# A two-layer recurrent decoder step on one core: norm statistics by a product with ones, the first embedding projection moved to the start, and the state-space constants made in pieces

## The chip, the core and the metric

The kernel runs on one core of a Trainium2 chip. The metric is the device time of one execution in microseconds (us). The profile shows five engines that run their own instruction lists and wait for each other through semaphores: TensorE (PE: matmuls, with its weight loads shown apart as PEld), VectorE (DVE), ScalarE (ACT), GpSimd (POOL) and SyncE (SP), which here does nothing but issue transfers. Matmul results go into PSUM, everything else is in SBUF or in the chip's main memory (DRAM).

## The reference

One step of a decoder trunk with two layers over 576 columns: 512 positions of a prompt and 8 samples of 8 positions. The width is 1024. Each layer is a mixer, a squared-ReLU MLP and a gated embedding addition, each behind a norm:

```
def rmsnorm(x, g):
    y = x * rsqrt(mean(x * x, axis=-1) + EPS)
    return y * g

for i in range(2):
    hn = rmsnorm(h, norm_mix[i])
    h = h + mixer_i(hn)                       # layer 0: mLSTM and retention; layer 1: HGRN2 and S5
    hn = rmsnorm(h, norm_ff[i])
    h = h + square(relu(hn @ w_ff1[i])) @ w_ff2[i]
    gate = sigmoid(rmsnorm(h, norm_ple[i]) @ w_ple_gate[i])
    h = h + gate * (p[i] @ w_ple_proj[i])     # p[i]: an input, 256 wide
y = rmsnorm(h, norm_final)
```

The S5 half of layer 1 is a complex diagonal state space of 32 groups with 64 states: from A, log_dt, B and C it needs the powers of exp(dt A), the scaled B, and products of them. These are constants: they hang on no activation.

## The kernel before

h is held transposed, as eight tiles of 128 rows (features) by 576 columns. Every large product is one of 219 *units*: 512 KB of weights that SP fetches (`wr`, L223), that ACT copies into a rounded part `wh` (L226), and whose remainder `wl` DVE or POOL forms (L227). Activations are split in the same way into `xh` (ACT, L270, with the norm's weight g multiplied in) and `xl` (DVE, L271). Each product is then three matmuls (wh·xh, wh·xl, wl·xh, L235) for each of two halves of 288 columns, into a `pb` bank of PSUM. One output tile of 128 rows with 1024 inputs is 48 matmuls, one with 256 inputs is 12.

The norm's factor r is not needed by the matmul, since it is a number for each column: it is multiplied in when the result leaves PSUM (for the MLP: `fu` L398 on DVE, relu times r, then ACT squares it, L399, and it is split again into `uh` and `ul`, L267 and L268). So the statistic is computed beside the first matmuls that use the norm. ACT squares the eight tiles (L304), POOL and DVE add them up into two tiles `sqa` (L305). A function `make` (L315) then does:

- ten matmuls of `sqa` with a column of ones (L322; in two parts for each of five blocks of columns), which give the sum for each column, the columns standing on the partitions;
- on DVE a square root's inverse by a bit trick and three Newton steps on 128x5 values (L323 to L331: 13 small instructions);
- five matmuls (L328) that spread the result over 128 partitions, and two copies into r (L330 on ACT, L331 on DVE).

There are six such norms: mix0, ff0, ple0 in layer 0, mix1, ff1, ple1 in layer 1. (The profile counts a matmul's two hardware passes, so the chain shows the ten and the five as 20 and 10.) The last norm is done otherwise, in `finish`, and is not touched.

`load` (L336) fetches the eight tiles of h and the unit of the first mixer's gate. `ple` (L417) runs two units of `w_ple_proj` on the embedding (eight outputs of 12 matmuls), lets ACT halve them into `prj` (L426), and then forms the norm and the gate. `ff` (L386) has four blocks b; each is eight units of w_ff1 and eight of w_ff2. A dictionary of hooks (block, 0 or 1, unit) calls other work between its units: in layer 0 the constants of S5. `late` at (0,0,4) makes all tables at once (L901 and the functions it calls: `pexp`, `cmul`, `s5_phases` with `unit_length`), some 170 small DVE instructions. `elem` (L1047) multiplies the tables with B and C in six large POOL instructions for each quarter ct of the groups (L1059 to L1061), the first at (0,1,0); `s5_turn` makes rotations on DVE; `prod` (L1065) has the PE products of them (L1074, L1075).

The order of every engine's list is not the order of the code: a scheduler that simulates the program (`schedule_with_timeline_sim=True`) lays each engine's instructions out; `high_priority(400)` around `make`, and the hooks, only tell it when something may come. Each engine then works through its list strictly in order.

Of the kernel before, what the change touches and what calls it, by code (L numbers as in the profile page):

```python
# [9 lines left out]
F32 = mybir.dt.float32  # L10
# [160 lines left out]
class K:  # L171
    def __init__(self, ctx, tc, A, units):
        self.ctx, self.tc, self.nc, self.A, self.units = ctx, tc, tc.nc, A, units
        nc = self.nc
        e = ctx.enter_context
        self.cp = e(tc.tile_pool(name="cp", bufs=1))
        self.rp = e(tc.tile_pool(name="rp", bufs=1))
        self.xp = e(tc.tile_pool(name="xp", bufs=8))
        self.wp = e(tc.tile_pool(name="wp", bufs=2))
        self.np_ = e(tc.tile_pool(name="np", bufs=2))  # L180
        self.nn = 0
        self.vec = self.cp.tile([P, NV], F32, name="vec")
        nc.scalar.dma_start(self.vec, A["vec"])
        self.one = self.cp.tile([P, 1], F32, name="one")
        nc.vector.memset(self.one, 1.0)
        self.eps = self.cp.tile([P, 1], F32, name="eps")
        nc.vector.memset(self.eps, EPS)
        nc.scalar.preload_act_table(AF.Exp)
# [11 lines left out]
        self.sud, self.yd = dram("sud", NT), dram("yd", NT)  # L200
        self.Rd = dram("Rd", 3 * 512)
        self.PR = self.rp.tile([P, 32], F32, name="s5PR")
        self.PI = self.rp.tile([P, 32], F32, name="s5PI")
        self.h = [self.rp.tile([P, NT], F32, name=f"h{k}") for k in range(KD)]
# [82 lines left out]
            ins = self.newton(r, m, t)  # L287
        return ins

    def norm(self, g, first=None):  # L290


        nc = self.nc
        xs = []
        r = self.np_.tile([P, NT], F32, name="r", tag="r", bufs=1)
        acc = [self.np_.tile([P, NT], F32, name="sqa", tag="sqa") for _ in range(2)]
        for k in range(KD):
            xs.append(self.split(self.h[k], self.v(g, k), first if k < 4 else None))
            i = int(k >= 5)
            if k in (0, 5):  # L300
                nc.scalar.activation(acc[i], self.h[k], AF.Square)
            else:
                t = self.np_.tile([P, NT], F32, name="sq", tag="sq")
                nc.scalar.activation(t, self.h[k], AF.Square)  # L304
                (nc.vector if i else nc.gpsimd).tensor_tensor(acc[i], acc[i], t, ALU.add)  # L305
        done = []

        def stat():
            if not done:
                done.append(1)  # L310
                with self.tc.high_priority(400):
                    make()
            return r

        def make():  # L315
            st = self.np_.tile([P, 3, 5], F32, name="rst", tag="rst")
            m, t, c = st[:, 0], st[:, 1], st[:, 2]
# [5 lines left out]
            nc.vector.tensor_scalar(m[:, 0:4], ps[:, 0:4], 1.0 / D, EPS, ALU.mult, ALU.add)  # L323
            nc.vector.tensor_scalar(m[:NS, 4:5], ps[:NS, 4:5], 1.0 / D, EPS, ALU.mult, ALU.add)
            self.stat_done = self.rsqrt(c, m, t)
            pa, pz = self.pmt(), self.pmt()
            for i, (t0, tn) in enumerate(TT):
                nc.tensor.matmul(pa[:, t0:t0 + tn] if i < 4 else pz[:, :tn], c[:tn, i:i + 1].to_broadcast([tn, P]),  # L328
                                 self.ident[:tn, :tn], start=True, stop=True)
            nc.scalar.copy(r[:, :NP], pa)  # L330
            nc.vector.tensor_copy(r[:, NP:], pz[:, :NS])  # L331

        return xs, stat


    def load(self):  # L336
        for k in range(KD):
            self.nc.sync.dma_start(self.h[k], self.A["hT"][k])
            if k == 0:
                self.gate_w = self.unit("gate")  # L340
        self.nc.sync.dma_start(self.cc, self.A["c0"][:, :NCC])

    def finish(self, n0, gate, pt):

# [41 lines left out]
    def ff(self, l, hooks={}):  # L386
        nc = self.nc
        xs, r = self.norm(f"ff{l}")
        with self.tc.tile_pool(name=f"ff{l}", bufs=12) as up, self.tc.tile_pool(name=f"fa{l}", bufs=3) as ap:
            for b in range(4):  # L390
                us = []
                for n in range(8):
# [11 lines left out]
                if b == 3:  # L404
                    self.xple = []
                    for k in range(2):
                        t = ap.tile([P, NT], F32, name="pin", tag="fu")
                        nc.sync.dma_start(t, self.A["pT"][l, k])
                        self.xple.append(self.split(t))
# [416 lines left out]
    def mix0(self):  # L826
        nc, tc = self.nc, self.tc
        with ExitStack() as st:
# [8 lines left out]
            xs, r = self.norm("mix0")  # L837
# [63 lines left out]
    def s5_tables(self, sp):  # L901
# [6 lines left out]
        Ar, Ai, ld = s5a[:, 0:32], s5a[:, 32:64], s5a[:, 64:96]  # L908
        dt, mag, x, n, r = (self.tiny(f"s5_{i}") for i in range(5))
        self.pexp(dt, ld)  # L910
        tt(x, dt, Ar, ALU.mult)
        self.pexp(mag, x)
        tt(x, dt, Ai, ALU.mult)
        ts(n, x, 1.0 / (2 * math.pi), MAGIC, ALU.mult, ALU.add)
        ts(n, n, MAGIC, None, ALU.subtract)
# [9 lines left out]
        nc.scalar.activation(r, x, AF.Sin)  # L925
        tt(pr[:, 1], mag, r, ALU.mult)
        tt(pi[:, 1], mag, n, ALU.mult)

        zr, zi, de, t = (self.tiny(f"s5z_{i}") for i in range(4))
        tt(de, Ar, Ar, ALU.mult)  # L930
# [10 lines left out]
        tt(t, x, Ai, ALU.mult)  # L941
        tt(zi, zi, t, ALU.subtract)
        tt(zi, zi, de, ALU.mult)
        tb = sp.tile([P, 8, 32], F32, name="s5tb")
# [8 lines left out]
        powers(pr, pi, 1)  # L953

        PR, PI = self.PR, self.PI
        nc.vector.tensor_copy(PR, pr[:, 8])
# [4 lines left out]
        ts(W1[64:], pi[64:], -1.0, None, ALU.mult)  # L961
        ts(W2[:64], pi[:64], -1.0, None, ALU.mult)
        ts(W2[64:], pr[64:], -1.0, None, ALU.mult)
        Y1, Y2 = sp.tile([P, 8, 32], F32, name="s5y1"), sp.tile([P, 8, 32], F32, name="s5y2")
        yr, yi = sp.tile([P, 8, 32], F32, name="s5yr"), sp.tile([P, 8, 32], F32, name="s5yi")
        b8 = lambda a: a.unsqueeze(1).to_broadcast([P, 8, 32])
        self.cmul(yr, yi, pr[:, 0:8], pi[:, 0:8], b8(zr), b8(zi), tb)
        nc.vector.tensor_copy(Y1[:64], yr[:64])
# [4 lines left out]
        self.s5_phases(sp, mag, r, n)  # L973
        return W1, W2, Y1, Y2

    def unit_length(self, c, s, q, t):
# [10 lines left out]
    def s5_phases(self, sp, mag, co, si):  # L987
# [9 lines left out]
        for k in range(8):  # L997
# [2 lines left out]
            c, s = o  # L1000
            if k > 1:
                self.unit_length(c, s, a, b)

    def s5_turn(self, sp, ct):

# [23 lines left out]
    def s5_hooks(self, st):  # L1029
# [4 lines left out]
        W = {}  # L1034

        def tables():
            self.bounds(sp)
            W["t"] = self.s5_tables(sp)
# [4 lines left out]
            nc.gpsimd.tensor_copy(self.lev, lev)  # L1043
            self.zer = sp.tile([16, 4, 112], F32, name="s5zero")
            nc.gpsimd.memset(self.zer, 0.0)

        def elem(ct):  # L1047
            W1, W2, Y1, Y2 = W["t"]
# [41 lines left out]
                if j:  # L1090
                    nc.sync.dma_start(rows[:, :, :j * 16], self.zer[:, :, :j * 16])

        def late():
            with self.tc.issue_after(self.stat_done.ins):
                tables()

        hooks = {(0, 0, 4): late}
        for ct in range(4):
            hooks[ct, 1, 3] = lambda ct=ct: self.s5_turn(sp, ct)
        for ct in range(4):  # L1100
            hooks[ct, 1, 0] = lambda ct=ct: elem(ct)
            if ct < 3:
                hooks[ct + 1, 0, 4] = lambda ct=ct: prod(ct, 0)
                hooks[ct + 1, 0, 6] = lambda ct=ct: prod(ct, 1)
        hooks[3, 1, 5] = lambda: prod(3, 0)
        hooks[3, 1, 7] = lambda: prod(3, 1)
        return hooks
# [294 lines left out]
def build(tc, A, units):  # L1402
    with ExitStack() as ctx:
        k = K(ctx, tc, A, units)
        k.load()
        with k.psum(2):
            k.mix0()
        with k.psum(3):
# [103 lines left out]
```

## Time and profile before

| | us |
|---|---|
| time, median of 3 runs | 1719.27 (1718.98 to 1720.6) |
| the profiled execution: its own time | 1719.25 |
| its span, first to last instruction | 1717.5 |
| PE busy | 1653.2 (96%) |
| DVE busy | 987.3 (57%) |
| ACT busy | 591.2 (34%) |
| POOL busy | 306.6 (18%) |

The mean granted clock of TensorE is 0.982 of full. A busy PE here means that some matmul is in flight; the matmuls of one unit follow each other at a fixed pitch, and their records overlap, so a record's own length is longer than its share of the time. The chain of waits names, for each moment, the work that the end of the program hung on; a piece "PE pb L235 x59" in it is 59 matmul records one behind the other.

### The profile page before, as it was taken

What the parts mean: (1) busy time and instruction counts of PE and PEld (TensorE: products, weight loads), DVE (VectorE), ACT (ScalarE), POOL (GpSimd) and SP (SyncE); (2) the same over time, 40 slices, a digit from 0 to 9 for tenths busy, and PEclk for the clock granted to TensorE, in tenths of its full rate; (3) what the DMA queues carried; (4) which work ended last, traced back from release to release, by engine and by line L of the source; (5) the groups of instructions that cost most, each with busy time, mean ns of one, the idle gap of its engine ahead of it and who ended that gap; (6) DMA issues with size and microseconds to landing.
All of it is one profiled execution on the core that took longest, in us unless ns stands there. A gap on an engine that the chain in (4) does not pass through costs nothing.

```text
span 1717.5 us, 29186 instructions
## 1 busy us (share of the span) xinstructions
PE 1653.2 (96%) x12129; PEld 1592.1 (93%) x12129; DVE 987.3 (57%) x1839; ACT 591.2 (34%) x931; POOL 306.6 (18%) x252
## 2 busy tenths in 40 slices
PE   7999999999899999999999799989999999999996
PEld 7989899999899999999999788979999999999996
DVE  7977656658835445365456787486532433334446
ACT  5333222344123132234443254352431322223344
POOL 3311223110302003021023464231100000000100
PEclk9999999999899999999999899899999999999998
DMA  5222222223223324243236322512222222223222
GB/s 188 96 88 99 81 77 89 87 89 99 93 87 119 100 84 134 75 136 110 78 94 205 111 84 71 139 65 67 71 87 86 79 82 87 86 75 101 86 74 68
DMA packets 75428, 164.21 MB, mean 96 GB/s; under 512 B 28832, under 2 KB 33824, under 8 KB 75168
## 3 DMA queue, kind: packets, MB, share of 16 engines
q1 hardware_dynamic: 74856, 161.84, 29.1%
q8 instruction: 95, 1.56, 0.4%
q10 hardware_dynamic: 440, 0.52, 0.1%
q14 instruction: 37, 0.30, 0.1%
HBM read 140.55 MB, written 21.77 MB: 95 GB/s over the span
## 4 chain that ended last, share of the span: by engine, by line
PE 83%; DVE 9%; ACT 3%; DMA 2%; issue 2%; SPq 1%; DVEq 0%; ACTq 0%
PE pb L235 73%; PE pm L706 1%; PE pm L476 1%; PE pm L726 1%; DVE e L1312 1%; PE pm L322 1%; DVE e L1314 1%; PE pm L1075 1%; PE pm L818 1%; PE pm L743 0%; DMA s5U<-yd 0%; PE pm L328 0%; PE pm L820 0%; PE pm L1074 0%; DVE wl L227 0%
## 5 line engine op out<-in xcount | busy, mean ns | idle before, releaser
L235 PE MATMUL pb<-xh,wh 128*128 128x288 f32 x2480 | 547.4, 301 | 21.6 <-ACT wh L226 10.4
L235 PE MATMUL pb<-xl,wh 128*128 128x288 f32 x2480 | 546.0, 300 | 3.0 <-DVE xl L271 3.0
L235 PE MATMUL pb<-xh,wl 128*128 128x288 f32 x2480 | 546.1, 300 | 0.0
L226 ACT CAST wh<-wr 128x1024 fp32r<-128x1024 f32 x219 | 229.9, 1050 | 804.3 <-PE pb L235 701.1
L235 PEld LDWEIGHTS pb<-xh,wh 128*128 128x128 f32 x2480 | 405.1, 191 | 29.8 <-issue 12.2
L235 PEld LDWEIGHTS pb<-xl,wh 128*128 128x128 f32 x2480 | 405.7, 191 | 11.3 <-issue 6.5
L235 PEld LDWEIGHTS pb<-xh,wl 128*128 128x128 f32 x2480 | 405.3, 191 | 6.1 <-issue 4.8
L227 DVE TENSOR_TENSOR wl<-wr,wh 128x1024 fp32r<-128x1024 f32 x199 | 249.5, 1254 | 15.7 <-ACT wh L226 5.6
L235 PE MATMUL pb<-uh,wh 128*128 128x288 f32 x1024 | 220.6, 298 | 8.3 <-ACT uh L267 8.3
L235 PE MATMUL pb<-ul,wh 128*128 128x288 f32 x1024 | 220.8, 297 | 0.0
L235 PE MATMUL pb<-uh,wl 128*128 128x288 f32 x1024 | 220.7, 297 | 0.0
L235 PEld LDWEIGHTS pb<-uh,wh 128*128 128x128 f32 x1024 | 165.9, 190 | 8.9 <-ACT uh L267 8.5
L415 DVE TENSOR_TENSOR h<-h,pb 128x576 f32<-128x576 f32 x64 | 48.3, 754 | 218.4 <-PE pb L235 218.4
L235 PEld LDWEIGHTS pb<-ul,wh 128*128 128x128 f32 x1024 | 166.0, 190 | 0.0
L235 PEld LDWEIGHTS pb<-uh,wl 128*128 128x128 f32 x1024 | 165.9, 190 | 0.0
L398 DVE SCALAR_TENSOR_TENSOR fu<-pb,r 128x576 f32<-128x576 f32 x64 | 48.3, 757 | 184.3 <-PE pb L235 184.1
L305 POOL TENSOR_TENSOR sqa<-sqa,sq 128x576 f32<-128x576 f32 x24 | 40.5, 1689 | 536.6 <-ACT sq L304 536.4
L227 POOL TENSOR_TENSOR wl<-wr,wh 128x1024 fp32r<-128x1024 f32 x20 | 50.5, 2529 | 99.2 <-ACT wh L226 98.3
L268 DVE TENSOR_TENSOR ul<-fu,uh 128x576 fp32r<-128x576 f32 x64 | 50.2, 785 | 9.2 <-ACT uh L267 8.9
L1059 POOL TENSOR_TENSOR s5ET<-s5bc,s5y 128x1024 f32<-128x1024 f32 x4 | 9.5, 2384 | 251.0 <-PE pm L1075 206.9
L271 DVE SCALAR_TENSOR_TENSOR xl<-h,vec,xh 128x576 fp32r<-128x576 f32 x48 | 43.3, 911 | 17.9 <-ACT xh L270 17.9
L704 POOL TENSOR_TENSOR Vm<-V,cc 64x384 f32<-64x384 f32 (+3 forms) x36 | 31.7, 892 | 100.4 <-ACT V L688 62.0
(454 smaller groups left out, 1639.9 us busy)
## 6 DMA issues: line engine op xcount, KB each, us to landing
wr<-in_w_dram SPq DMA_DIRECT2D x219, 512.0 KB, 3.5
sR<-Rd SPq DMA_DIRECT2D x12, 256.0 KB, 2.9
h<-in_hT_dram SPq DMA_DIRECT2D x8, 288.0 KB, 5.4
Gd<-s5G SPq DMA_DIRECT2D x4, 576.0 KB, 3.8
sG<-Gd SPq DMA_DIRECT2D x8, 288.0 KB, 5.9
out_yT_dram<-h SPq DMA_DIRECT2D x16, 144.0 KB, 1.9
s_in<-in_Cst_dram SPq DMA_DIRECT2D x4, 516.0 KB, 5.7
out_Cs_dram<-s_in SPq DMA_DIRECT2D x4, 516.0 KB, 3.1
```

The source lines that it names most:

```text
L226: nc.scalar.copy(hi, raw)
L227: (nc.gpsimd if self.lo_pool else nc.vector).tensor_tensor(lo, raw, hi.bitcast(F32), ALU.subtract)
L235: mm(ps[:, j, :HALF], a, b[:, j * HALF:(j + 1) * HALF], start=first and a is wh and b is xh, stop=last and a is wl)
L268: nc.vector.tensor_tensor(lo, src, hi.bitcast(F32), ALU.subtract)
L271: nc.vector.scalar_tensor_tensor(lo, src, scale, hi.bitcast(F32), ALU.mult, ALU.subtract)
L305: (nc.vector if i else nc.gpsimd).tensor_tensor(acc[i], acc[i], t, ALU.add)
L322: nc.tensor.matmul(ps[:tn, i:i + 1], acc[j][:, t0:t0 + tn], self.one, start=j == 0, stop=j == 1)
L398: nc.vector.scalar_tensor_tensor(self.sv(u), self.pv(ps), 0.0, self.sv(r()), ALU.max, ALU.mult)
L415: nc.vector.tensor_tensor(self.sv(self.h[n]), self.sv(self.h[n]), self.pv(ps), ALU.add)
L476: nc.tensor.transpose(dst, src[:n, t0:t0 + tn], self.ident[:n, :n])
L704: nc.gpsimd.tensor_tensor(Vm, V[:NS, 4, :n].unsqueeze(1).to_broadcast([NS, b1 - b0, n]), self.vmask[:, b0:b1].unsqueeze(2).to_broadcast([N ...
L706: nc.tensor.matmul(ps, Kt[:NS, 4], Vm.rearrange("p b n -> p (b n)"), start=True, stop=True)
```

## The change

Three things are changed.

**The statistic.** The two sums `sqa` are added on DVE, ACT takes a rounded copy `sqh`, DVE the remainder `sql`, and PE multiplies both by a 128x128 tile of ones: four matmuls of 288 columns, whose result already stands on all partitions. r comes from it as exp(-ln(m)/2) on ACT and one Newton step on DVE, now on 128x576 values. The matmuls L322 and L328 and the 128x5 steps go. For mix0, POOL's part in the additions goes to DVE.

**The first embedding projection.** The two units of `w_ple_proj` of layer 0 move from `ple` to `load`, before everything else. The eight results are written to DRAM (`prd`) by DMAs on POOL's queue and fetched again in `ple` by eight DMAs on SP's queue. Its split of the input (L366 after) moves too; layer 1 keeps its place.

**The S5 constants.** `s5_tables` and `s5_phases` become generators; hooks at (0,0,4) to (0,1,6) take two pieces each, (0,1,7) the rest. The hooks of `elem`, `s5_turn` and `prod` move later (elem(0) from (0,1,0) to (1,0,0)).

```
     def make():
-            nc.vector.memset(m, 1.0)
-            ps = self.pmt()
-            for i, (t0, tn) in enumerate(TT):
...
-                    nc.tensor.matmul(ps[:tn, i:i + 1], acc[j][:, t0:t0 + tn], self.one, start=j == 0, stop=j == 1)
...
-            self.stat_done = self.rsqrt(c, m, t)
...
-                nc.tensor.matmul(pa[:, t0:t0 + tn] if i < 4 else pz[:, :tn], c[:tn, i:i + 1].to_broadcast([tn, P]),
-                                 self.ident[:tn, :tn], start=True, stop=True)
-            nc.scalar.copy(r[:, :NP], pa)
-            nc.vector.tensor_copy(r[:, NP:], pz[:, :NS])
+            hi, lo = (self.np_.tile([P, NT], F32R, name=f"sq{i}", tag="sq") for i in "hl")
+            tt(acc[0], acc[0], acc[1], ALU.add)
+            last = nc.scalar.copy(hi, acc[0])
+            if tables:
+                with self.tc.issue_after(last.ins):
+                    nc.scalar.preload_act_table_set("natural_log_exp_and_others")
+            tt(lo, acc[0], hi.bitcast(F32), ALU.subtract)
+            ps = [self.pmt()[:, :HALF] for _ in range(2)]
+            for b in (hi, lo):
                 for j in range(2):
+                    nc.tensor.matmul(ps[j], self.ones, b[:, j * HALF:(j + 1) * HALF], start=b is hi, stop=b is lo)
+            m, q = acc
+            for j in range(2):
+                s = slice(j * HALF, (j + 1) * HALF)
+                nc.scalar.activation(r[:, s], ps[j], AF.Ln, bias=self.eps, scale=1.0 / D)
+                nc.vector.tensor_scalar(m[:, s], ps[j], 1.0 / D, EPS, ALU.mult, ALU.add)
+            nc.scalar.activation(r, r, AF.Exp, scale=-0.5)
+            self.stat_done = self.newton(r, m, q)
     def load(self):
+            with self.tc.high_priority(60):
+                self.embed_in(0, lp, nc.sync)
+                ws = [self.unit("col2", "w_ple_proj", 0, 0, 0)]
...
+            for n2 in range(2):
+                for n in range(4):
+                    ps = self.cols(ws[n2], self.xple, (2 * n, 2 * n + 1))
+                    o = lp.tile([P, NT], F32, name="po", tag="po", bufs=3)
+                    with self.tc.high_priority(60):
+                        nc.scalar.mul(self.sv(o), self.pv(ps), 0.5)
+                    nc.gpsimd.dma_start(self.prd[n2 * 4 + n], o)
     def ple(self, l, xq=None):
+            if l == 0:
+                for n in range(8):
+                    o = pp.tile([P, NT], F32, name=f"prj{n}")
+                    nc.sync.dma_start(o, self.prd[n])
+                    prj.append(o)
-            for n2 in range(2):
+            for n2 in range(2 if l else 0):
     def s5_hooks(self, st):
-        hooks = {(0, 0, 4): late}
+        hooks = {(0, j // 8, j % 8): piece for j in range(4, 15)}
+        hooks[0, 1, 7] = lambda: piece(99)
         for ct in range(4):
-            hooks[ct, 1, 0] = lambda ct=ct: elem(ct)
...
+                hooks[ct + 1, 0, 0] = lambda ct=ct: elem(ct)
```

What the scheduler makes of this, at three places.

PE at the start of the program, before: the gate's unit (wh_122, wl_123) is the first thing on it.

```order
L235 MATMUL pb<-xh,wh_122 128x288 x2
L235 MATMUL pb<-xl,wh_122 128x288 x2
L235 MATMUL pb<-xh,wl_123 128x288 x2
L235 MATMUL pb<-xh,wh_122 128x288 x2
L235 MATMUL pb<-xl,wh_122 128x288 x2
L235 MATMUL pb<-xh,wl_123 128x288 x2
```

PE after the change, rows 41 to 51: the end of the projection's second unit (wh_162, wl_163; the 96 matmuls of both units stand ahead), then the statistic of mix0, then the gate's unit, which is now wh_237.

```order
L238 MATMUL pb<-xh,wh_162 128x288 x2
L238 MATMUL pb<-xl,wh_162 128x288 x2
L238 MATMUL pb<-xh,wl_163 128x288 x2
L238 MATMUL pb<-xh,wh_162 128x288 x2
L238 MATMUL pb<-xl,wh_162 128x288 x2
L238 MATMUL pb<-xh,wl_163 128x288 x2
L331 MATMUL pm<-sqh,ones 128x288 x2
L331 MATMUL pm<-sql,ones 128x288 x2
L238 MATMUL pb<-xh,wh_237 128x288 x2
L238 MATMUL pb<-xl,wh_237 128x288 x2
L238 MATMUL pb<-xh,wl_238 128x288 x2
```

All 96 matmuls of the projection now stand ahead of the first matmul that uses h, and the statistic stands ahead of all of the gate's unit rather than inside it.

DVE in the MLP of layer 0, before, from the seventh unit of its first block (the `fu` in the fourth row) on. `s5y_4580` and `s5y_4581` are the tables for which POOL's elem(0) waits.

```order
L971 COPY s5y_4581<-s5yr 64x256
L899 TENSOR_TENSOR s5yi<-s5yi,s5tb 128x256
L894 TENSOR_TENSOR s5yr<-s5p_4597 128x32
L398 SCALAR_TENSOR_TENSOR fu<-pb,r 128x576
L969 COPY s5y_4580<-s5yi 64x256
L970 TENSOR_SCALAR s5y_4581<-s5yi 64x256
L896 TENSOR_TENSOR s5yr<-s5yr,s5p_w 128x32
L227 TENSOR_TENSOR wl_4959<-wr_4956,wh_4958 128x1024
L897 TENSOR_TENSOR s5yi<-s5p_4597,s5p_4598 128x32
```

The same place after the change (rows 716 to 726); the tables are now `s5y_4978` and `s5y_4979`.

```order
L1007 COPY s5y_4978<-s5yi 64x256
L1008 TENSOR_SCALAR s5y_4979<-s5yi 64x256
L927 TENSOR_TENSOR s5yr<-s5yr,s5p_w 128x32
L928 TENSOR_TENSOR s5yi<-s5p_5051,s5p_5052 128x32
L929 TENSOR_TENSOR s5p_w<-s5p_5052,s5p_5051 128x32
L1018 TENSOR_TENSOR s5p_5049<-s5yr 128x32
L930 TENSOR_TENSOR s5yi<-s5yi,s5p_w 128x32
L1019 TENSOR_TENSOR s5p_5050<-s5yi 128x32
L428 SCALAR_TENSOR_TENSOR fu<-pb,r 128x576
L1020 TENSOR_TENSOR s5p_5049<-s5p_5049,s5p_5050 128x32
L230 TENSOR_TENSOR wl_4991<-wr_4988,wh_4990 128x1024
```

The two writes of the tables move from just behind the `fu` of the seventh unit to eight rows ahead of it; six of the small 128x32 steps have come ahead of it with them. Between this `fu` and the next (the eighth unit's) stand 22 rows before and 22 after, of the same kinds.

PE at the norm ff0, before: in the MLP's second unit (wh_4257) the five small matmuls that spread the result stand; the column sums L322 stand 28 rows earlier.

```order
L235 MATMUL pb<-xl,wh_4257 128x288 x2
L235 MATMUL pb<-xh,wl_4258 128x288 x2
L235 MATMUL pb<-xh,wh_4257 128x288 x2
L328 MATMUL pm<-cc,rst 128x128 x4
L328 MATMUL pm<-cc,rst 128x64
L235 MATMUL pb<-xl,wh_4257 128x288 x2
```

The same norm after the change, again in the MLP's second unit (here wh_4400).

```order
L238 MATMUL pb<-xh,wh_4400 128x288 x2
L331 MATMUL pm<-sqh,ones 128x288 x2
L238 MATMUL pb<-xl,wh_4400 128x288 x2
L238 MATMUL pb<-xh,wl_4401 128x288 x2
L238 MATMUL pb<-xh,wh_4400 128x288
L331 MATMUL pm<-sql,ones 128x288 x2
L238 MATMUL pb<-xh,wh_4400 128x288
L238 MATMUL pb<-xl,wh_4400 128x288 x2
L238 MATMUL pb<-xh,wl_4401 128x288 x2
```

PE came to the statistic at three places of this norm before (one column sum, the nine others, the spreading); now it comes once, in two parts with a few matmuls between them.

## Rows read from the trace of the kernel before

**Rows 1.** The page: span; busy time and share by engine, count of instructions.
```profile
span 1717.5 us, 29186 instructions
PE 1653.2 (96%) x12129; PEld 1592.1 (93%) x12129; DVE 987.3 (57%) x1839; ACT 591.2 (34%) x931; POOL 306.6 (18%) x252
```
**Rows 2.** Chain of waits, 365 to 540 us (start, length, what): norm ff0.
```profile
372.83 0.11 PE pm L322 x2
...
382.88 1.78 PE pm L322 x18
...
391.64 1.25 PE pm L328 x10
```
**Rows 3.** The chain in that stretch, further on: S5 tables, then 96 matmuls.
```profile
425.65 0.77 DVE fu L398
...
443.72 0.68 DVE fu L398
...
445.86 73.38 PE pb L235 x534
...
521.41 12.99 PE pb L235 x96
```
**Rows 4.** The chain in later stretches: norms ple0, ff1 and ple1.
```profile
826.36 1.78 PE pm L322 x18
...
834.45 1.25 PE pm L328 x10
...
1224.93 1.78 PE pm L322 x18
...
1638.32 1.78 PE pm L322 x18
```
**Rows 5.** DVE timeline, 368 to 396 us: the wait for ff0's column sums.
```profile
384.70 0.16 DVE L323 TENSOR_SCALAR rst<-pm 128x4 f32<-128x4 f32 x1 [4.82 <-PE pm L322]
```
**Rows 6.** The chain at the start of the program.
```profile
7.16 0.78 ACT xh L270
7.93 0.58 ACT sq L304
...
28.02 0.75 DVE gR L492
...
42.76 9.29 PE pb L235 x68
52.05 0.31 PE pm L548 x5
```
**Rows 7.** Engines by stretch: busy us (records) of each, granted clock, DMA share.
```profile
0.00:10.00 10.00, 3.69 (x13) 3.12 (x14) 3.21 (x9) 6.42 (x9) 3.56 (x12) 1.00 0.82 278
10.00:20.00 10.00, 6.82 (x43) 5.56 (x42) 10.00 (x10) 7.70 (x12) 6.65 (x4) 1.00 0.79 316
...
440.00:460.00 20.00, 14.14 (x91) 14.14 (x92) 19.31 (x96) 3.44 (x4) 2.61 (x1) 0.74 0.31 102
```
**Rows 8.** Groups by line: mean ns of one is behind the busy time.
```profile
L226 ACT CAST wh<-wr 128x1024 fp32r<-128x1024 f32 x219 | 229.9, 1050 | 804.3 <-PE pb L235 701.1
...
L235 PE MATMUL pb<-uh,wh 128*128 128x288 f32 x1024 | 220.6, 298 | 8.3 <-ACT uh L267 8.3
...
L426 ACT ACTIVATE prj<-pb 128x576 f32<-128x576 f32 x16 | 10.4, 649 | 9.9 <-PE pb L235 9.8
```
**Rows 9.** DVE timeline, 425 to 446 us: small S5 steps.
```profile
430.18 0.17 DVE L898 TENSOR_TENSOR s5p_w<-s5p,s5p 128x32 f32<-128x32 f32 x1
...
433.33 2.27 DVE L982 TENSOR_TENSOR s5p<-s5p,s5p 128x32 f32<-128x32 f32 x1
...
440.06 2.65 DVE L894 TENSOR_TENSOR s5yr<-s5yr 128x32 f32<-128x32 f32 x1
```
**Rows 10.** POOL timeline: first and last of six elem(0) instructions.
```profile
426.81 3.40 POOL L1059 TENSOR_TENSOR s5ET<-s5bc,s5y 128x1024 f32<-128x1024 f32 x1 [44.10 <-DVE s5y L969]
...
440.06 2.61 POOL L1061 TENSOR_TENSOR s5G<-s5G,s5t 128x1152 f32<-128x1152 f32 x1
```

More of the change, by code (lines that the diff above doesn't have):

```diff
@@ L185, in __init__ @@
         nc.vector.memset(self.one, 1.0)
+        self.ones = self.cp.tile([P, P], F32R, name="ones")
+        nc.vector.memset(self.ones.bitcast(F32), 1.0)
         self.eps = self.cp.tile([P, 1], F32, name="eps")
         nc.vector.memset(self.eps, EPS)
-        nc.scalar.preload_act_table(AF.Exp)
+        nc.scalar.preload_act_table_set("natural_log_exp_and_others")
         self.cc = self.cp.tile([P, NCC], F32, name="cc")
@@ L200, in __init__ @@
         self.sud, self.yd = dram("sud", NT), dram("yd", NT)
+        self.prd = [dp.tile([P, NT], F32, name=f"prd{i}") for i in range(8)]
         self.Rd = dram("Rd", 3 * 512)
@@ L288, in rsqrt, with norm @@
         return ins
-    def norm(self, g, first=None):
+    def norm(self, g, first=None, dve=False, tables=True):
         nc = self.nc
@@ L304, in norm @@
                 nc.scalar.activation(t, self.h[k], AF.Square)
-                (nc.vector if i else nc.gpsimd).tensor_tensor(acc[i], acc[i], t, ALU.add)
+                (nc.vector if i or dve else nc.gpsimd).tensor_tensor(acc[i], acc[i], t, ALU.add)
         done = []
@@ L324, in make @@
-            nc.vector.tensor_scalar(m[:NS, 4:5], ps[:NS, 4:5], 1.0 / D, EPS, ALU.mult, ALU.add)
-            self.stat_done = self.rsqrt(c, m, t)
-            pa, pz = self.pmt(), self.pmt()
-            for i, (t0, tn) in enumerate(TT):
-                nc.tensor.matmul(pa[:, t0:t0 + tn] if i < 4 else pz[:, :tn], c[:tn, i:i + 1].to_broadcast([tn, P]),
-                                 self.ident[:tn, :tn], start=True, stop=True)
-            nc.scalar.copy(r[:, :NP], pa)
-            nc.vector.tensor_copy(r[:, NP:], pz[:, :NS])
+            tt = nc.vector.tensor_tensor
@@ L333, in norm @@
+            m, q = acc
[5 more added lines that the diff above has]
+            self.stat_done = self.newton(r, m, q)
         return xs, stat
     def load(self):
[L337 to L340, printed above, removed]
@@ L341, in load @@
-        self.nc.sync.dma_start(self.cc, self.A["c0"][:, :NCC])
+        nc = self.nc
+        with self.tc.tile_pool(name="lp", bufs=2) as lp:
+            with self.tc.high_priority(60):
+                self.embed_in(0, lp, nc.sync)
+                ws = [self.unit("col2", "w_ple_proj", 0, 0, 0)]
+            for k in range(KD):
+                nc.sync.dma_start(self.h[k], self.A["hT"][k])
+                if k == 3:
+                    ws.append(self.unit("col2", "w_ple_proj", 0, 512, 0))
+            nc.sync.dma_start(self.cc, self.A["c0"][:, :NCC])
+            for n2 in range(2):
[5 more added lines that the diff above has]
+                    nc.gpsimd.dma_start(self.prd[n2 * 4 + n], o)
+                if n2 == 0:
+                    self.gate_w = self.unit("gate")
@@ L343, in finish, with embed_in @@
+    def embed_in(self, l, pool, eng, xp=None):
+        self.xple = []
+        for k in range(2):
+            t = pool.tile([P, NT], F32, name="pin", tag="fu")
+            eng.dma_start(t, self.A["pT"][l, k])
+            self.xple.append(self.split(t, pool=xp or pool))
     def finish(self, n0, gate, pt):
@@ L403, in ff @@
                     us.append((hi, lo))
[L404 to L409, printed above, removed]
+                if b == 3 and l == 1:
+                    self.embed_in(l, ap, nc.sync, self.xp)
                 for n in range(8):
@@ L836, in mix0 @@
             self.mixed = []
-            xs, r = self.norm("mix0")
+            xs, r = self.norm("mix0", dve=True, tables=False)
             inner = st.enter_context(ExitStack())
@@ L910, in s5_tables @@
         self.pexp(dt, ld)
+        yield
         tt(x, dt, Ar, ALU.mult)
         self.pexp(mag, x)
+        yield
         tt(x, dt, Ai, ALU.mult)
@@ L927, in s5_tables @@
         tt(pi[:, 1], mag, n, ALU.mult)
+        yield
         zr, zi, de, t = (self.tiny(f"s5z_{i}") for i in range(4))
@@ L943, in s5_tables @@
         tt(zi, zi, de, ALU.mult)
+        yield
         tb = sp.tile([P, 8, 32], F32, name="s5tb")
@@ L951, in powers @@
                 self.cmul(r_[:, lo:hi], i_[:, lo:hi], r_[:, base:lo], i_[:, base:lo], br, bi, tb[:, :m])
-        powers(pr, pi, 1)
+                yield
+        yield from powers(pr, pi, 1)
         PR, PI = self.PR, self.PI
@@ L963, in s5_tables @@
         ts(W2[64:], pr[64:], -1.0, None, ALU.mult)
+        yield
         Y1, Y2 = sp.tile([P, 8, 32], F32, name="s5y1"), sp.tile([P, 8, 32], F32, name="s5y2")
@@ L967, in s5_tables @@
         self.cmul(yr, yi, pr[:, 0:8], pi[:, 0:8], b8(zr), b8(zi), tb)
+        yield
         nc.vector.tensor_copy(Y1[:64], yr[:64])
@@ L972, in s5_tables @@
         self.uc, self.us, self.turn_t = yr, yi, tb
-        self.s5_phases(sp, mag, r, n)
+        yield from self.s5_phases(sp, mag, r, n)
         return W1, W2, Y1, Y2
@@ L1002, in s5_phases @@
                 self.unit_length(c, s, a, b)
+            yield
     def s5_turn(self, sp, ct):
@@ L1036, in tables @@
         def tables():
-            self.bounds(sp)
-            W["t"] = self.s5_tables(sp)
             self.sD = sp.tile([16, 32], F32, name="s5D")
@@ L1045, in tables, with piece @@
             nc.gpsimd.memset(self.zer, 0.0)
+            self.bounds(sp)
+            yield
+            W["t"] = yield from self.s5_tables(sp)
+        pieces = tables()
+        def piece(n=2):
+            for _ in range(n):
+                next(pieces, None)
         def elem(ct):
@@ L1091, in prod @@
                     nc.sync.dma_start(rows[:, :, :j * 16], self.zer[:, :, :j * 16])
-        def late():
-            with self.tc.issue_after(self.stat_done.ins):
-                tables()
-        hooks = {(0, 0, 4): late}
+        hooks = {(0, j // 8, j % 8): piece for j in range(4, 15)}
+        hooks[0, 1, 7] = lambda: piece(99)
         for ct in range(4):
-            hooks[ct, 1, 3] = lambda ct=ct: self.s5_turn(sp, ct)
-        for ct in range(4):
-            hooks[ct, 1, 0] = lambda ct=ct: elem(ct)
             if ct < 3:
-                hooks[ct + 1, 0, 4] = lambda ct=ct: prod(ct, 0)
-                hooks[ct + 1, 0, 6] = lambda ct=ct: prod(ct, 1)
+                hooks[ct + 1, 0, 0] = lambda ct=ct: elem(ct)
+                hooks[ct + 1, 0, 3] = lambda ct=ct: self.s5_turn(sp, ct)
+                hooks[ct + 1, 0, 5] = lambda ct=ct: prod(ct, 0)
+                hooks[ct + 1, 0, 7] = lambda ct=ct: prod(ct, 1)
+        hooks[3, 1, 0] = lambda: elem(3)
+        hooks[3, 1, 3] = lambda: self.s5_turn(sp, 3)
         hooks[3, 1, 5] = lambda: prod(3, 0)
@@ L1404, in build @@
         k = K(ctx, tc, A, units)
-        k.load()
+        with k.psum(3):
+            k.load()
         with k.psum(2):
```

4 lines of the change are left out of this document (1 added, 3 removed).

## The prediction

> **What bounds the kernel now.** I read the page first: of a span of 1717.5 us PE is busy for 1653.2, 96%, and no other engine passes 57% [rows 1]. So a microsecond taken off PE's list is a microsecond of time in most stages, and work moved to DVE or ACT is free where they have room. Then I followed the chain of waits through each place that the change touches: the norms in the middle of the program [rows 2, 4], the S5 tables [rows 3], the start [rows 6]. The reader is to see in it which steps of the old statistic stand on PE itself, and where PE is not the bound: at the start, where PE worked for only 3.69 + 6.82 = 10.5 of the first 20 us [rows 7], and between two `fu` of the first MLP [rows 3]. Last come the timelines of DVE and POOL in that second place, which show why PE stood still there [rows 9, 10].
>
> The unit of account is the pitch of a large matmul: 96 of them in 12.99 us, 0.135 us each [rows 3].
>
> The sum below is made against the profiled execution: span 1717.5 us, its own time 1719.25, so 1.75 us lie outside the span. The median of the runs, 1719.27, is the same number for this purpose.
>
> **The statistic.** Per norm, PE's list loses one column sum (0.11 us), nine more (1.78) and the spreading (1.25), together 3.14 us, all on the chain [rows 2]; the other norms show the same steps with the same lengths [rows 4]. It gains four matmuls of 288 columns, the size of the large ones: 4 x 0.135 = 0.54. That leaves 2.6 us per norm. Five norms lie where PE is the chain (ff0, ple0, mix1, ff1, ple1): -13.0 us.
>
> Cover. The new steps beside PE are wider: on DVE an addition, a remainder, two halves of m and three Newton steps, about six full-width instructions at 0.75 (the price of one over 576 columns [rows 6]), 4.5 us where thirteen small ones and a copy stood; on ACT a copy, two Ln, an Exp and a table load, some 4 us at ACT's 0.58 to 0.78 per tile [rows 6] and more for the load. At ff0 DVE waited 4.82 us for the column sums alone [rows 5], so the room is there. The result must be ready when the first `fu` wants it: before, 384.66 (end of the sums) plus DVE's steps plus the spreading at 391.64, so at about 393. Now there is one visit to PE and about 4 us behind it. From the position of the four matmuls on PE (in the second unit of the MLP, where the spreading stood before) r comes at about 390 to 394 by these prices, at the earliest 3 us before the old one. If it came 3 us late at all five, DVE would hold a `pb` bank, of which there are several; I price that at 0 and keep 5 x 1 us as the end on the bad side. On the good side nothing beyond 3.14 per norm can be had: -15.7.
>
> **The projection.** Its 96 matmuls are 96 x 0.135 = 13.0 us that leave `ple`, where PE is the chain. At the start they do not come free. The two units' weights and the input now stand ahead of h on SP's queue, and ACT has to do more before the statistic of mix0 can be formed: two splits of the input (2 x 0.67), the two weight copies (2 x 1.05 [rows 8]), eight pairs of `xh` and `sq` (8 x 1.25, rather under the first pair's 0.78 + 0.58 [rows 6]), three evictions that come before the copy of the sum (3 x 0.65 [rows 8]), the gate's weight copy (1.05) and that copy (0.67): 17.1 us from about 6.5, so 23 to 24 at most, 22 if the copies fall into waits. PE has the projection's first tiles in this time; the last two of its eight tiles need a `pb` bank that only the fourth and fifth eviction free, behind the copy. 22.3 + 2 x 0.65 + one tile of 12 matmuls (1.6) gives 25.2 to 25.6, the statistic 0.5 more: 26.1.
>
> From there PE has 260 large matmuls to the point that the chain of before reached at 52.05 [rows 6], 260 x 0.135 = 35.1 us without a gap: 61.2, that is 9.1 later than before. The gate's first DVE step on r, at 28.02 before [rows 6], comes at about 33 to 34, some 5.5 later, so DVE's own chain, which bound the stretch up to 42.76 [rows 6], is covered by PE's shift. I take 9.5 for the start, since some of DVE's waits up to 42.76 will stay, and the net is -13.0 + 9.5 = -3.5. Bounds: 8.7 if every gap closes (-4.3); and 13.0 if none of the idle time at the start is used (0). Mix0's old statistic, 3.1 us on PE, is inside this count. The eight reloads of 288 KB in front of the second layer-0 gate's weights are wanted some 16 us after they are issued; a tile of h of that size took 5.49 us at the busiest time. I price them at 0.
>
> **The S5 constants.** The chain stands on DVE from 425.65 to 445.86 [rows 3]: `fu` of the seventh unit at 425.65, of the eighth at 443.72, 18.1 us apart where a unit of 48 matmuls is 6.5. PE was idle for 8.3 us of that, waiting for ACT's split behind the late `fu` [rows 8], and then ran for a while at the half clock (granted 0.74 in 440 to 460, 91 records in 14.14 us where 0.135 each makes 12.3 [rows 7], so 1.8 us). The number of DVE instructions is not the cause: a 128x32 step takes 0.17 us, but some took 2.27 or 2.65 [rows 9]. Six of them did, 2.02 to 2.65 us, each ending with one of the six instructions of POOL's elem(0), which ran without a break from 426.81 to 442.67 [rows 10]. A DVE step on two SBUF operands waits there for POOL's current instruction.
>
> The Trainium skill, "SBUF — State Buffer", section "SBUF: two separate sides", calls the port that DVE and GpSimd share an exclusive lock held for the whole instruction, the other side being fully blocked. The trace agrees: blocked steps end when POOL's does. By that rule cutting the DVE work into pieces does nothing for the stall as long as elem(0) runs beside it; without it the pieces would remove it.
>
> So what counts is when elem(0) starts. It waits for the two tables alone, and the hook that issues it later does not hold it back: in POOL's list it follows the same instructions as before. In DVE's list the tables' last writes have moved from behind the seventh `fu` to eight rows ahead of it, so elem(0) starts about 2.3 us earlier against the units (six small steps at 0.1 to 0.2, waiting for PE's cadence the rest). Between the seventh and eighth `fu` stand again 22 rows, and POOL still needs 15.9 us. All six POOL instructions therefore still come before the eighth `fu`; I put the stall at 7.2 instead of 8.3 and the clock loss as it was: -1.0. Bounds: 0, and 8.3 + 1.8 = -10.1.
>
> **Sum.** -13.0 - 3.5 - 1.0 = -17.5; 1717.5 - 17.5 = 1700.0, with 1.75 outside it: 1701.8, about **1702 us**.
>
> **The rivals.**
>
> *The stall goes.* If POOL gets its inputs so much earlier, or DVE slips its steps in between POOL's so often, that the eighth `fu` comes on PE's cadence, 9.1 us more go: 1702 - 9 = 1693. For it: the pieces start from the fifth unit on, and a few steps at 0.17 do slip through between blocked ones [rows 9]. Against it: POOL's 15.9 us do not fit between two `fu` 6.5 us apart.
>
> *The start eats the projection.* PE's list now begins with matmuls that alternate with evictions by an ACT that is the bound, so PE may stand for a microsecond or two several times up to 22 us. Then the statistic comes at 28 instead of 26, and if PE falls to the half clock there, as behind the stall [rows 7], 2 us more are lost: shift 13 to 14 instead of 9.5, so 1706. For it: ACT's 17 us in a row; against it: before, PE idled in those 20 us just as often.
>
> *POOL's queue holds DVE (slower).* The eight transfers of the results are issued on POOL, in the stretch in which DVE is the bound. If each holds DVE as a POOL instruction does, 2.65 us [rows 9], that is 8 x 2.65 = 21.2: 1702 + 21 = 1723. It decides only from (17.5 + 3.4)/8 = 2.6 us for each. Against it: DVE waits for ACT at many points there, and no POOL arithmetic stands in these issues; no row shows their price.
>
> *The pieces do nothing at all* is inside the forecast: it would be 1703.
>
> **How the numbers follow.** Forecast 0.52, the stall goes 0.21, the start eats 0.24, POOL's queue 0.03. What can be told from no change is 0.2%, 3.4 us. The first three are all faster by more than 11 us; I leave 0.03 for no change (the second half of the costs at once) and 0.02 for slower. Range: from 1690 (the stall gone, and the good end of the statistic) to 1711 (the start at its bad end, 1706, and 5 us for a late r). The scheduler also laid out the unchanged layer-1 mixer anew, which I cannot price; that widens the range and does not move its middle.
>
> **What would show it.** In the changed profile: L331 as four matmuls of about 0.135 in the chain, no second visit of PE to the norm, and r before the first `fu`; PE's first 96 records in the first 26 us and gR at 33 to 34; no projection between the MLP and the gate of layer 0; and, in the first MLP, POOL's six instructions in a row with DVE steps of over 2 us beside them and a PE wait of about 7 us before the eighth unit's products. The prediction is wrong if that wait is gone or has grown, if PE waits at a new place for r, or if the granted clock falls to 1.2 GHz in the first 40 us.

## The result and the profile after

The changed kernel takes 1699.17 us (median of 4 runs, 1697.35 to 1700.08) where the kernel before takes 1719.44 beside it: a ratio of 0.988 (95% interval 0.9863 to 0.9897), 20 us less. Run again later (after_again below), its ratio is 0.9885 (0.9862 to 0.9909). The forecast was 1702, in a range from 1690 to 1711.

The page of the profile, the rows that answer to [rows 1], and a queue that was not there before:

```profile
span 1697.9 us, 28934 instructions
...
PE 1622.4 (96%) x11973; PEld 1564.9 (92%) x11973; DVE 1004.9 (59%) x1796; ACT 604.4 (36%) x952; POOL 308.0 (18%) x256
...
q0 software_dynamic: 640, 2.36, 0.3%
```

PE has lost 31 us of work and the span only 20: PE now stands still for longer. q0 carries the eight transfers of the projection (8 x 288 KB).

To see where the time went I compared the start of the same instruction in both timelines, after minus before. This table is worked out from the timelines of DVE:

| up to | lag, us | step | forecast of the step |
|---|---|---|---|
| first use of r in layer 0 (gR) | +12.5 | | about +5.5 |
| end of the first mixer (last h of its output) | +14.9 | +14.9 | +9.5 |
| fifth `fu` of the first MLP | +11.4 | -3.5 (norm ff0) | -2.6 |
| ninth `fu` | +11.8 | +0.4 (S5 tables) | -1.0 |
| last h of the first MLP | +11.5 | -0.3 | 0 |
| second z of ple0 | -3.5 | -15.0 (projection, norm) | -15.6 |
| end of the second mixer | -9.0 | -5.5 (norm mix1) | -2.6 |
| second `fu` of the second MLP | -12.0 | -3.0 (norm ff1) | -2.6 |
| last h of the second MLP | -15.6 | -3.6 | 0 |
| last z of ple1 | -19.5 | -3.8 (norm ple1) | -2.6 |

The total is 2.8 us from the forecast, but by terms that missed in both directions. The lags are read from one profile of each kernel, and at the start they are not exact: a second profile of the changed kernel (after_again) has +11.2 and +13.9 in the first two rows, and before_ones (below), which does the work of the kernel before, has +1.8 and +3.0. The steps behind the first mixer agree within 0.9 us in the two profiles of the changed kernel.

**The norms.** The chain at ff0, beside [rows 2]: one visit to PE.

```profile
399.79 0.26 PE pm L331 x2
...
400.71 0.26 PE pm L331 x2
```

0.53 us stand where 3.14 stood, as forecast, and PE did not wait for r there. In ple1 it is the same (L331 at 1624.13 for 0.26).

**The start.** The chain of the start, beside [rows 6]:

```profile
21.45 2.38 DMA prd<-po
...
24.93 5.35 DMA prd<-po
...
40.55 0.75 DVE gR L523
```

ACT's timeline there, and then PE's, with what ended the idle time in brackets:

```profile
23.99 1.73 ACT L361 ACTIVATE po<-pb 128x576 f32<-128x576 f32 x3
...
30.36 1.36 ACT L361 ACTIVATE po<-pb 128x576 f32<-128x576 f32 x2 [1.46 <-DMA prd<-po]
```

```profile
31.77 0.53 PE L331 MATMUL pm<-sqh,ones 128*128 128x288 f32 x2 [3.70 <-ACT po L361]
```

The eviction `po` has three buffers. The seventh eviction writes a buffer whose content must first have left for DRAM, and this transfer took 5.35 us from its issue on POOL at 24.93. ACT itself stood idle for it for 1.46 us only. A larger part of the delay lies in the order of ACT's list: the fourth to sixth evictions stand behind the gate's weight copy and the copy of the sum, and come at 23.99 (po8, below, shows the list with more buffers). The statistic of mix0 waits for the last eviction, and so comes at 31.8 and not at 26.1; the forecast let it follow the last tile at once. Behind the 3.70 us of idle time PE ran at the lower of its two clock levels, 1.2 GHz, for some 3 us (0.24 us from one matmul to the next where 0.13 is usual; granted 0.91 in 20 to 40).

**The S5 tables.** DVE's timeline, beside [rows 9]:

```profile
438.19 2.08 DVE L928 TENSOR_TENSOR s5yi<-s5p,s5p 128x32 f32<-128x32 f32 x1
...
442.92 0.75 DVE L428 SCALAR_TENSOR_TENSOR fu<-pb,r 128x576 f32<-128x576 f32 x1
...
448.24 0.75 DVE L428 SCALAR_TENSOR_TENSOR fu<-pb,r 128x576 f32<-128x576 f32 x1
...
451.14 3.26 DVE L230 TENSOR_TENSOR wl<-wr,wh 128x1024 fp32r<-128x1024 f32 x1
454.33 2.59 DVE L930 TENSOR_TENSOR s5yi<-s5yi,s5p_w 128x32 f32<-128x32 f32 x1
```

POOL's timeline, beside [rows 10]:

```profile
436.08 2.13 POOL L1105 TENSOR_TENSOR s5ET<-s5bc,s5y 128x1024 f32<-128x1024 f32 x1 [39.47 <-DVE s5y L1007]
...
448.80 2.27 POOL L1105 TENSOR_TENSOR s5G<-s5bc,s5w 128x1152 f32<-128x1152 f32 x1 [6.07 <-DMA s5bc<-in_s5bc_dram]
...
453.40 3.47 POOL L1107 TENSOR_TENSOR s5G<-s5G,s5t 128x1152 f32<-128x1152 f32 x1
```

The six instructions did not run in a row. The first three started when the tables were there and held DVE as forecast: the seventh `fu` came 11.5 us behind the sixth, where a unit takes 6.4. The other three waited 6.07 us for their input transfer, so the eighth `fu` came through, 5.3 us behind the seventh. But then they held the next `wl` (3.26 us for 1.22) and the split of the eighth unit. PE waited 1.46 us for the `wl` behind the late seventh `fu`, and then for this split:

```profile
457.87 0.85 PE L238 MATMUL pb<-ul,wh 128*128 128x288 f32 x2 [6.60 <-DVE ul L271]
```

```profile
440.00:460.00 20.00, 11.77 (x78) 11.06 (x78) 19.52 (x49) 4.72 (x6) 10.64 (x5) 0.82 0.27 96
```

PE is idle for 8.2 us of these 20 (before: 2.4 + 5.9 in 420 to 460). The wait before the eighth unit's products has moved from the first half of its split (`uh`) to the second (`ul`), and, with the 1.46 us, kept its size.

### The profile page after: what moved, and what is told of

It reads as the page before. It is cut to its first block, busy times and chain, and to the rows that moved or that the text cites. A ratio compares the mean times of both kernels' runs of the same rounds, so it can differ in the third digit from the quotient of the medians.

```text
span 1697.9 us, 28934 instructions
## 1 busy us (share of the span) xinstructions
PE 1622.4 (96%) x11973; PEld 1564.9 (92%) x11973; DVE 1004.9 (59%) x1796; ACT 604.4 (36%) x952; POOL 308.0 (18%) x256
## 4 chain that ended last, share of the span: by engine, by line
PE 82%; DVE 10%; ACT 3%; DMA 3%; issue 2%; SPq 0%; POOL 0%; ACTq 0%; DVEq 0%; POOLq 0%
PE pb L238 73%; PE pm L737 1%; PE pm L507 1%; DVE wl L230 1%; DVE e L1356 1%; DVE e L1358 1%; PE pm L1367 1%; PE pm L757 1%; PE pm L1121 1%; DMA s5U<-yd 1%; ACT xh L273 1%; PE pm L774 0%; DMA prd<-po 0%; DVE s5w L1204 0%; PE pm L849 0%
## 5 line engine op out<-in xcount | busy, mean ns | idle before, releaser
L238 PE MATMUL pb<-xh,wh 128*128 128x288 f32 x2480 | 544.0, 300 | 31.0 <-ACT wh L229 12.4
L308 POOL TENSOR_TENSOR sqa<-sqa,sq 128x576 f32<-128x576 f32 x20 | 32.8, 1640 | 502.1 <-ACT sq L307 481.3
L429 ACT ACTIVATE fu<-fu 128x576 f32<-128x576 f32 x64 | 43.8, 685 | 10.6 <-DVE fu L428 10.0
```

The costliest lines, as they stand in the source:

```text
L238: mm(ps[:, j, :HALF], a, b[:, j * HALF:(j + 1) * HALF], start=first and a is wh and b is xh, stop=last and a is wl)
L308: (nc.vector if i or dve else nc.gpsimd).tensor_tensor(acc[i], acc[i], t, ALU.add)
L429: nc.scalar.activation(u, u, AF.Square)
```

## The experiments

Verdicts are ratios against the kernel before, run on the same chip; lags are against the profile of before, as in the table. The first four kernels shared one chip, after_again, elem_late, both and before_ones a second; once_late ran on a third.

**One part at a time.** Theory A took the sizes from the table above; theory B those of the forecast. Three kernels, each the changed kernel with parts taken back (line numbers of the text are of the changed kernel).

n_only: the norm alone, `load`, `ple`, the S5 tables and all hooks as before. Here and in norm_s5, POOL's part in the additions of mix0 comes back too.

> The kernel before with the new norm statistic alone (projection in ple, S5 tables at once as before). Theory A (read off the two traces: each norm gives 2.9 to 3.5 us of PE, the layer-1 mixer behind an earlier r some 2 us more, the projection's move costs 2, the pieces give nothing): about -17 us against before without the pitch drift in the second MLP, so 1702, and down to 1698 if the short pitch (6.24 us a unit) shows here too; lag of the first fu of layer 0 about -3 and the S5 wait as long as before. Theory B (the forecast's sizes: norms -13.0, projection -3.5, S5 -1.0): 1706.

norm_s5: the projection back in `ple`.

```
-            with self.tc.high_priority(60):
-                self.embed_in(0, lp, nc.sync)
-                ws = [self.unit("col2", "w_ple_proj", 0, 0, 0)]
...
-            for n2 in range(2 if l else 0):
+            for n2 in range(2):
```

> The changed kernel with the projection put back into ple. Theory A: the move of the projection cost 15.1 us at the start and gave 13.0, so without it 1697, 2 us faster than the changed kernel, with gR back at about 28. Theory B: the move gave 3.5 us, so 1702.5 here.

norm_proj: the tables at once, the hooks as before.

```
-        hooks = {(0, j // 8, j % 8): piece for j in range(4, 15)}
-        hooks[0, 1, 7] = lambda: piece(99)
+        def late():
+            with self.tc.issue_after(self.stat_done.ins):
+                for _ in tables():
+                    pass
+        hooks = {(0, 0, 4): late}
```

> The changed kernel with the S5 tables made at once, hooks as before. Theory A: the first MLP loses as much either way (lag before and behind it 11.6 and 11.8), so 1699, as the changed kernel. Theory B: 1 us slower, 1700; the rival in which the pieces had freed the eighth unit: 1708.

| kernel | ratio (95%) | lag gR | end of first mixer | ninth `fu` | last z |
|---|---|---|---|---|---|
| n_only | 0.9861 (0.9846 to 0.9876) | +5.5 | +6.4 | +0.7 | -18.8 |
| norm_s5 | 0.9891 (0.9875 to 0.9906) | +4.8 | +4.6 | +1.9 | -16.9 |
| norm_proj | 0.9850 (0.9834 to 0.9867) | +12.8 | +15.5 | +9.4 | -20.8 |
| changed kernel | 0.9885 (0.9862 to 0.9909; on the second chip) | +12.5 | +14.9 | +11.8 | -19.5 |

The norm alone gives as much as the three changes together. Beside the runs of before, n_only takes 23.9 us less (theory A 17 to 21, B 13), norm_s5 19.5 (A 22, B 17) and norm_proj 26.3 (A 20, B 19): neither theory fits all three.

Three findings went against theory A. First, the projection's move is not a loss of 2 us and looks worth about 2: the last z of norm_proj lies 2.0 before that of n_only, and of the changed kernel 2.6 before that of norm_s5; the times point the same way, but their intervals (0.9850 and 0.9861) overlap. Second, theory A had put the whole start to the projection, while 5.5 us of the lag at gR (4.8 in norm_s5) come with the new norm alone: mix0's statistic has more steps on ACT and DVE in a row, and there no matmul hides them. ACT could start on r at 27.98, r was ready at 33.5, and PE stood idle for 6.08 us (granted clock 0.74 in 20 to 40):

```profile
27.98 0.89 ACT L336 ACTIVATE r<-pm,eps 128x288 f32<-128x288 f32 x2 [5.64 <-PE pm L331]
```

```profile
35.20 0.82 PE L238 MATMUL pb<-xh,wh 128*128 128x288 f32 x2 [6.08 <-DVE gi L506]
```

Third, the pieces, with the later hooks that came with them, cost something: between the fifth and the ninth `fu` n_only gains 2.2 us and norm_proj 2.6, where the kernels with pieces gain nothing (+0.2 and +0.4). In 420 to 480 PE stands idle for 5.1 and 4.9 us with the tables at once (8.3 in the kernel before, which theory A expected to stay), for 7.8 and 8.2 with the pieces. In the times the cost reads as 0.3% (0.9861 to 0.9891, 0.9850 to 0.9885, the second pair from two chips), with intervals that just overlap.

**The buffers.** po8:

```
-                    o = lp.tile([P, NT], F32, name="po", tag="po", bufs=3)
+                    o = lp.tile([P, NT], F32, name="po", tag="po", bufs=8)
```

> The changed kernel with eight instead of three buffers for the halved projection, so that no eviction waits for a transfer to DRAM. Theory A (the transfers, 2.4 and 5.4 us in the chain, hold the buffers, and by them the PSUM banks and the statistic): PE's idle times of 1.6 us at 23 and 3.7 at 28 shrink to under 1 together, gR at 35 to 37 instead of 40.5, time 1694 to 1696. Rival (ACT's list is the bound there, the transfer only came last): gR moves by under 1 us, 1698 to 1699.

Ratio 0.983 (0.9815 to 0.9844). gR lags by 5.0 instead of 12.5 and comes at 33.0, earlier than theory A had it. ACT's timeline (the fourth eviction), PE's and the chain:

```profile
19.67 0.64 ACT L361 ACTIVATE po<-pb 128x576 f32<-128x576 f32 x1
```

```profile
25.72 0.53 PE L331 MATMUL pm<-sqh,ones 128*128 128x288 f32 x2 [1.42 <-ACT po L361]
```

```profile
26.52 25.61 PE pb L238 x192
```

The statistic comes at 25.7 (the forecast said 26.1), and PE then runs without a gap. The three buffers were the cause, the rival falls. They act in two ways that this edit does not separate: by the wait for a transfer, and by the order that the scheduler gives ACT's list, in which the fourth eviction now stands ahead of the gate's weight copy and the copy of the sum, 5.3 us behind the first eviction and not 7.7.

Not all of the 7.5 us at gR is theirs: already the first eviction, before any buffer is used again, comes 2.0 us earlier in this profile (14.36, changed kernel 16.31). The kernel `both` below against elem_late, with first evictions 0.2 us apart, gives 6.2 us. The lag at the end of the first mixer is 7.8.

**POOL's hold.** after_again is the changed kernel itself, as a base; elem_late puts the input transfers of `elem` behind the last weight fetch:

```
+                with self.tc.issue_after(self.wdma.ins):
                     nc.sync.dma_start(bc, self.A["s5bc"][ct][:, 2 * q:2 * q + 2])
```

> The changed kernel once more, on the chip and beside the runs of the kernel before that the next ones have, as their base: ratio 0.987 to 0.989 by all theories.

> The changed kernel; the input transfer of each elem stands behind the weight fetch that was issued last, so that POOL's six instructions start some 40 us later, when the phases are done. Theory A (the stall of the first MLP is POOL's hold on DVE's small steps, the pieces don't matter): no small DVE step over 1 us in 400 to 480, PE idle there under 1 us instead of 8.2, no half clock, 9 to 11 us less than the changed kernel, ratio about 0.982. Rival (DVE's list is too long there in itself): PE still waits 4 us or more, gain under 5.

after_again: 0.9885. elem_late: 0.9837 (0.9814 to 0.9861). POOL starts here:

```profile
476.11 2.04 POOL L1106 TENSOR_TENSOR s5ET<-s5bc,s5y 128x1024 f32<-128x1024 f32 x1 [79.12 <-DMA s5bc<-in_s5bc_dram]
```

and the stretch of the stall has no idle PE and no half clock:

```profile
440.00:460.00 20.00, 20.00 (x153) 20.00 (x152) 15.88 (x72) 4.75 (x6) 0.00 (x0) 1.00 0.26 80
```

The lag falls from 12.4 at the fifth `fu` to 2.3 at the ninth: 10 us, and the time is 9.1 us below after_again. No small DVE step in 400 to 480 takes over 0.5 us. In this profile the second mixer lost some 5 of the 10 (granted clock 0.58 in 940 to 960); it is the slowest of the four runs (1695.43, the lowest 1689.37), and what the second mixer does in the others I did not follow.

**Both, and the tables at once.**

> Eight buffers for the projection and the later elem together: the two gains add (each in a stage of its own), 14 to 17 us less than the changed kernel, ratio 0.978 to 0.980.

both (eight buffers and the later `elem`): 0.9783 (0.9761 to 0.9804), 1682.95 us. That is 17.9 us less than after_again; the two gains add (9.1 for elem_late, 9.5 by the ratios for po8), to a little more than expected. The lag is 6.4 at gR and 9.1 at the end of the first mixer (elem_late: 12.6 and 15.3). once_late is the same kernel with the tables made at once:

> As the kernel with eight buffers and the later elem, but the S5 tables made at once behind the statistic of the MLP's norm, as before, instead of in pieces. If POOL's hold on DVE was the whole cause of the stall (theory A), the pieces are worth nothing once elem stands elsewhere: ratio 0.976 to 0.981, lag at the ninth fu within 1 us of the lag at the first. If the pieces do matter by themselves (rival: DVE's list in one lump delays fu by several us), PE idles 3 us or more in 400 to 460 and the ratio is 0.980 or more.

0.9789 (0.9762 to 0.9815), 1683.6 us, and no idle PE in 400 to 480. The lag does not stay within 1 us, as expected, but falls from 5.5 at the first `fu` to -5.2 at the ninth; in `both` it falls from 6.0 to -3.8. That sign was set wrongly, since the kernel before, against which lags are taken, has its own stall between the two. So with `elem` out of the way it makes no difference that could be measured whether the tables come in pieces; the hold was the whole stall.

**The pitch.** before_ones asks for the cause of a gain that no term had (below):

```
+        self.ones = self.cp.tile([P, P], F32R, name="ones")
+        nc.vector.memset(self.ones.bitcast(F32), 1.0)
```

> The kernel before with the 128x128 tile of ones allocated and set, and not used: all later tiles of SBUF stand 512 bytes further. If the shorter pitch of 6.24 us a unit, which all kernels with the new norm show in the same blocks of the second MLP, hangs on where tiles stand, it shows here too and the time falls by 3 to 4 us; if it hangs on the work, all units stay at 6.40.

0.9996 (0.998 to 1.0013); all units stay at 6.40. Shifting the later tiles by 512 bytes is not it.

## Why the prediction was right, and where it was not

- *PE is the bound in the norms.* Right. 3.14 us against 0.53 on PE, as read; the term was undersized: from the point before each norm to the first uses of its r, the lag falls by 2.9 to 3.0 at ff0, ff1 and ple1, where 2.6 stood. I have no row for the other 0.3 to 0.4. What the table shows beyond that is the shorter pitch of the last section: some units behind ff0, and those of ple1, take 6.24 us instead of 6.40. Mix1 shows 5.5, and the reason stays open.
- *The projection is worth 13.0 us in `ple` and costs 9.5 at the start; net -3.5.* The first half holds: 15.0 with the norm, forecast 15.6. The second failed at one step: "the last two of its eight tiles need a `pb` bank that only the fourth and fifth eviction free", which counted the banks and ACT's list, but not that three `po` buffers are freed by transfers on POOL's queue, nor that the statistic waits for the eighth eviction (3.70 us; 1.42 in po8). I had priced these transfers only as issues on POOL. With eight buffers the statistic comes at 25.7 (po8) and 27.1 (both), gR at 33.0 and 34.4 (forecast 33 to 34), and the lag at the mixer's end is 7.8 and 9.1. The buffers cost about 6 us at the start. The count of 260 matmuls between the statistic and the point that the kernel before reached at 52.05 did not hold either: 192 stand there after the change, 240 in po8.
- *The shift belongs to the projection.* Partly wrong. In n_only the norm alone lags by 5.5 at gR and by 6.4 at the end of the first mixer. The forecast counted mix0's statistic inside the start and so had the sum, but not which edit owned it: with eight buffers the lag there is 7.8 and 9.1 (po8, both), with the norm alone 6.4 and 4.6 (n_only, norm_s5), so the projection itself adds 1.4 to 4.5 us.
- *The stall at the S5 tables is POOL's hold on DVE, and pieces do not cure it.* Right, and shown by elem_late and once_late. The size, -1.0, did not come: +0.4 in the lag, -0.4 in after_again, since the wait for the second input transfer split POOL's six instructions, and the second three hit the next unit's `wl` and split. The sentence "POOL's six instructions in a row" was wrong. That the pieces do nothing beside a running `elem` was not quite right either: with them the lag between the fifth and the ninth `fu` gains nothing, without them 2.2 and 2.6 us. The rule of the Trainium skill cited there (the page "SBUF — State Buffer", "SBUF: two separate sides") agrees with these runs: each blocked 128x32 step ends within 0.1 us of a POOL instruction, the blocked `wl` (3.26 us) 1.08 us behind one, and in 400 to 480 no step is long where POOL is idle.
- *The rivals.* "The start eats the projection" came nearly true in its number (shift 14.9; it had 13 to 14), by another mechanism; the half clock it named came too (0.91 in 20 to 40). By the prediction's own words a fall to 1.2 GHz in the first 40 us was a sign of being wrong, and for the start it was. "POOL's queue holds DVE" did not happen: an issue took 0.54 us on POOL and DVE had no long step beside it.
- *What came unforeseen.* 3.6 us in the body of the second MLP, some 3 in the second mixer. Without them the time would have been near 1706, so that the total came this near 1702 is in part luck.

## What to carry to other kernels

When work is moved to another place, count what frees each buffer it writes, not only the engines: a buffer that leaves by DMA is busy until the transfer has landed, and a pool that is too small can cost more through the order of an engine's list (here the fourth eviction, 2.4 us later counted from the first) than through the wait that the profile shows (1.46 us). Where small VectorE steps take ten times their usual length, look at GpSimd's timeline beside them before cutting the work up: starting the GpSimd work at another time gave 9 to 10 us, cutting the VectorE work beside it cost 2 to 3. And where several edits come together, the sum can be right with the parts wrong; one part at a time showed that one of three gave the gain.

## What was not expected of the hardware

The matmuls of the MLPs do not follow each other at one fixed pitch; they have two. In the kernel before the units of the second MLP take 6.40 us, apart from a few at the edges of a block. In every kernel with the new norm, the same 24 units of it take 6.24 (eight of w_ff2, the next block's eight of w_ff1, and eight of w_ff2 in the last block), with the same instructions and full clock. The same stretch before and after, records of PE in brackets:

```profile
1380.00:1400.00 20.00, 20.00 (x152) 20.00 (x151) 5.94 (x6) 3.15 (x3) 0.00 (x0) 1.00 0.27 93
```

```profile
1380.00:1400.00 20.00, 20.00 (x156) 20.00 (x155) 5.94 (x6) 3.15 (x3) 0.00 (x0) 1.00 0.28 91
```

24 x 0.16 = 3.8 us, which covers the 3.6 of the table. What sets the pitch stays open; before_ones excludes only one shift of the tiles. Two more things can be read from the traces. In the first MLP one and the same kernel has both pitches at the same place: the third to fifth `fu` follow each other in 6.24 us in the first profile of the changed kernel and in 6.40 in after_again, so where the tiles stand and what PE executes do not settle it. And in a long unit every fourth matmul starts 0.140 us behind the one before, the others 0.131; in a short one 0.132 and 0.128 alternate.

A transfer of 288 KB issued on POOL's queue took 2.4 to 5.6 us to land in the changed kernel. h had landed by then (at 15.4); weights were still being fetched, and the three slowest transfers (5.35 to 5.64) were issued within 1.1 us of each other.
